# Batched matrix product on one core: load order at the start, stores behind all loads, two outputs in the input's buffers

## The chip, the cores and the metric

The kernel runs on one NeuronCore of a Trainium2 chip. Five engines work side by side: TensorE (PE) multiplies, VectorE (DVE) rounds, transposes and copies, ScalarE (ACT) copies, GpSimd (POOL) does next to nothing here, and SyncE (SP) issues the transfers between the chip's main memory (HBM) and the core's working memory (SBUF). The transfers themselves are carried out by 16 DMA engines. TensorE writes its results into PSUM, a memory of 8 banks[...].

The metric is the device time of one execution in microseconds; lower is better. The profile is of a separate execution, and its span is from the first to the last instruction on the core.

## The reference

```python
def setup_inputs():
    batch, dim_i, dim_j, dim_k = 32, 256, 512, 384
    return {
        "x": np.random.randn(batch, dim_i, dim_j).astype(np.float32),
        "y": np.random.randn(batch, dim_j, dim_k).astype(np.float32),
    }

def reference(x, y):
    return np.einsum('bij,bjk->bik', x, y).astype(np.float32)
```

There are 32 independent products of a 256x512 matrix with a 512x384 matrix. The inputs are 16.8 MB (x) and 25.2 MB (y), the output 12.6 MB.

## The kernel before

Four batch entries form a group, so there are 8 groups, 0 to 7. Each entry of a group takes 32 of the 128 partitions. What is done for a group `n` is split into parts, each with a letter, and a plan lists the parts in program order:

- `x`, `y`: load the group's x (2 MB) or y (3 MB). Both are issued by SP.
- `T`: VectorE rounds x to float16 (one instruction) and transposes it (two instructions, or four for a "wide" group).
- `R`: VectorE rounds y to float16, in four instructions.
- `M`: TensorE multiplies, 128 products in two halves `e` of 64. Half `e` fills four PSUM banks, `(e, 0)` to `(e, 3)`.
- `C`: ScalarE copies banks to the output tile. `D`: VectorE copies the banks that are left to it.
- `S`: SP stores the output tile (1.5 MB).

```python
Q = 4
STEP = 4
O_BUFS = 5
WIDE_GROUPS = 6

PLAN = """
x0 x1 y0
T0 x2 y1
T1 R0 M0 C0 x3 y2
T2 D0 R1 M1 C1 x4 y3
T3 D1 R2 M2 C2 x5 y4
T4 D2 R3 M3 C3 x6 y5
T5 D3 R4 M4 C4 x7 S0 S1 S2 y6
T6 D4 R5 M5 C5 y7
T7 D5 R6 M6 C6 R7 M7 C7 D7 S3 S4 S5 S6 S7
"""
# ... (cut)
    x_pool = ctx.enter_context(tc.tile_pool(name="x_pool", bufs=2))
    y_pool = ctx.enter_context(tc.tile_pool(name="y_pool", bufs=2))
    xr_pool = ctx.enter_context(tc.tile_pool(name="xr_pool", bufs=1))
    xt_pool = ctx.enter_context(tc.tile_pool(name="xt_pool", bufs=3))
    yr_pool = ctx.enter_context(tc.tile_pool(name="yr_pool", bufs=2))
    o_pool = ctx.enter_context(tc.tile_pool(name="o_pool", bufs=O_BUFS))
# ... (cut)
    def width(n):
        return PQ if n < WIDE_GROUPS else 2 * PQ        # PQ = 32

    def on_vector(n, e, g):
        if n < WIDE_GROUPS:
            return (e, g) == (NE - 1, Q - 1)            # NE = 2
        return n == N - 1 and g % 2 == 1                # N = 8

    def load_x(n):
        x_of[n] = x_pool.tile([P, R, J], F32, name="x_sb")
        keep(nc.sync.dma_start(out=x_of[n], in_=x[...]))        # cut

    def transpose_x(n):
        x_r = xr_pool.tile([P, R, J], MM_DT, name="x_r")
        keep(nc.vector.tensor_copy(x_r, x_of.pop(n)))
        # ... transposes of x_r into xt_of[n] (cut)

    def round_y(n):
        y_sb = y_of.pop(n)
        yr_of[n] = yr_pool.tile([P, T, K], MM_DT, name="y_r")
        for a in range(0, T, STEP):                     # T = 16
            keep(nc.vector.tensor_copy(yr_of[n][:, a : a + STEP], y_sb[:, a : a + STEP]))

    def multiply(n):
        # ... (cut)
        o_of[n] = o_pool.tile([P, R, K], F32, name="o_sb")
        for e in range(NE):
            for g in range(Q):
                ps_of[n, e, g] = bank[e, g]
            for t in range(T):
                for g in range(Q):
                    s = slice(g * PQ, (g + 1) * PQ)
                    keep(nc.tensor.matmul(ps_of[n, e, g], xt[s, e, t // 2, :, t % 2], y_r[s, t],
                                          start=(t == 0), stop=(t == T - 1)))
```

A pool with `bufs=2` has two buffers. A new tile gets a buffer whose earlier tile has had its last use in program order, and the first instruction that writes the new tile waits for that use. A load of x is therefore held back by the rounding of an earlier x. Each engine takes its instructions in program order, and SP holds its queue while an issue waits.

A group below `WIDE_GROUPS` has its banks copied in pieces of 32 rows, four a bank; a wide group in pieces of 64 rows, two a bank.

Of the kernel before, what the change touches and what calls it, by code (L numbers as in the profile page):

```python
# [1 line left out]

# [4 lines left out]


MM_DT = mybir.dt.float16
F32 = mybir.dt.float32  # L10
P = 128


Q = 4
STEP = 4
O_BUFS = 5
WIDE_GROUPS = 6

PLAN = """
x0 x1 y0
T0 x2 y1
T1 R0 M0 C0 x3 y2
T2 D0 R1 M1 C1 x4 y3
T3 D1 R2 M2 C2 x5 y4
T4 D2 R3 M3 C3 x6 y5
T5 D3 R4 M4 C4 x7 S0 S1 S2 y6
T6 D4 R5 M5 C5 y7  # L30
T7 D5 R6 M6 C6 R7 M7 C7 D7 S3 S4 S5 S6 S7
"""


@with_exitstack
def kernel(
    ctx: ExitStack,
    tc: tile.TileContext,
    x: bass.AP,
    y: bass.AP,  # L40
    out: bass.AP,
):
    nc = tc.nc

    B, I, J = x.shape
    _, _, K = y.shape

    PQ = P // Q
    R = I // PQ
    T = J // PQ  # L50
    TW = T // 2
    NE = I // P
    N = B // Q
# [7 lines that stand above are left out]
    psum_pool = ctx.enter_context(  # L61
        tc.tile_pool(name="psum", bufs=1, space=bass.MemoryType.PSUM)
    )

    keep = tc.keep_in_program_order

    bank = {
        (e, g): psum_pool.tile([P, K], F32, name=f"o_ps_{e}_{g}") for e in range(NE) for g in range(Q)
    }

    x_of, y_of, xt_of, yr_of, ps_of, o_of = {}, {}, {}, {}, {}, {}

    def width(n):
        return PQ if n < WIDE_GROUPS else 2 * PQ

    def on_vector(n, e, g):
        if n < WIDE_GROUPS:  # L80
            return (e, g) == (NE - 1, Q - 1)
        return n == N - 1 and g % 2 == 1

    def load_x(n):
        x_of[n] = x_pool.tile([P, R, J], F32, name="x_sb")
        keep(
            nc.sync.dma_start(
                out=x_of[n],
                in_=x[n * Q : (n + 1) * Q].rearrange("g (p r) j -> (g p) r j", r=R),
            )  # L90
        )

    def load_y(n):
        y_of[n] = y_pool.tile([P, T, K], F32, name="y_sb")
        keep(
            nc.sync.dma_start(
                out=y_of[n],
                in_=y[n * Q : (n + 1) * Q].rearrange("g (q t) k -> (g q) t k", t=T),
# [8 lines that stand above are left out]
        xt_of[n] = xt_pool.tile([P, NE, TW, P], F32, name="xt_sb")  # L107
        b = width(n) // PQ
        src = x_r.bitcast(F32).rearrange("p (b h e) (q t) -> p b e t h q", b=b, e=NE, t=TW)
        dst = xt_of[n].rearrange("p e t (h s b) -> p b e t h s", s=PQ, b=b)  # L110
        for e in range(NE):
            for c in range(b):
                keep(nc.vector.transpose(dst[:, c, e], src[:, c, e]))  # L113
# [4 lines that stand above are left out]
        for a in range(0, T, STEP):  # L118
            keep(nc.vector.tensor_copy(yr_of[n][:, a : a + STEP], y_sb[:, a : a + STEP]))  # L119

    def multiply(n):
        xt = xt_of.pop(n).bitcast(MM_DT).rearrange("p e t (m c) -> p e t m c", c=2)
        y_r = yr_of.pop(n)
        o_of[n] = o_pool.tile([P, R, K], F32, name="o_sb")
        for e in range(NE):
            for g in range(Q):
                ps_of[n, e, g] = bank[e, g]
# [3 lines that stand above are left out]
                    keep(  # L131
                        nc.tensor.matmul(  # L132
                            ps_of[n, e, g],
                            xt[s, e, t // 2, :, t % 2],
                            y_r[s, t],
                            start=(t == 0),
                            stop=(t == T - 1),
                        )
                    )

    def collect(n, vector):
        w = width(n)
        per = P // w
        copy = nc.vector.tensor_copy if vector else nc.scalar.copy
        o = o_of[n].rearrange("p (u f) k -> p u f k", u=Q // per)
        for e in range(NE):
            for g in range(Q):
                if on_vector(n, e, g) != vector:
                    continue
                ps = ps_of.pop((n, e, g))  # L150
                a = g % per * w
                for h in range(per):
                    keep(copy(o[a : a + w, g // per, h * NE + e], ps[h * w : (h + 1) * w]))  # L153

    def store(n):
        w = width(n)
        per = P // w
        dst = out[n * Q : (n + 1) * Q].rearrange("(u g) (s f) k -> (g s) u f k", g=per, s=w)
        keep(
            nc.sync.dma_start(  # L160
                out=dst, in_=o_of.pop(n).rearrange("p (u f) k -> p u f k", u=Q // per)
            )
        )

    parts = {
        "x": load_x,
        "y": load_y,
        "T": transpose_x,
        "R": round_y,
        "M": multiply,  # L170
        "C": lambda n: collect(n, False),
        "D": lambda n: collect(n, True),
        "S": store,
    }
    for step in PLAN.split():
        parts[step[0]](int(step[1:]))


# [1 line left out]
_INS = ['x', 'y']  # L180
_OUTS = [((32, 256, 384), 'float32')]


# [23 lines left out]
```

## Time and profile before

The device time is 134.45 us (median of 3 runs, 134.24 to 134.48). The span of the profiled execution is 132.9 us.

| Engine | busy us | share of the span | instructions |
|---|---|---|---|
| TensorE, products | 61.5 | 46% | 1024 |
| TensorE, weight loads | 34.9 | 26% | 1024 |
| VectorE | 96.1 | 72% | 92 |
| ScalarE | 91.7 | 69% | 193 |

| Instruction | count | mean ns |
|---|---|---|
| ScalarE copy of a 32x384 piece | 168 | 470 |
| ScalarE copy of a 64x384 piece | 24 | 474 |
| VectorE copy of a piece | 32 | 556 |
| VectorE rounding of a quarter of y | 32 | 953 |
| VectorE rounding of x | 8 | 2292 |
| VectorE transpose of half of x | 12 | 2001 |
| VectorE transpose of a quarter of x | 8 | 1075 |

The DMA engines moved 54.68 MB at a mean of 412 GB/s: 41.94 MB are read from HBM and 12.58 MB written. In the profile's lines L87 is the load of x, L96 the load of y, L106 the rounding of x, L113 its transposition, L119 the rounding of y, L132 the products, L153 the copies out of PSUM and L160 the store. A line of a timeline gives start and duration in us, engine, line, operation, output and input, and in brackets the idle time before it and what ended it. "SPq" is SP issuing a transfer, not the transfer. A row of the slices divides the span into 40 equal parts of 3.3 us; a digit is the busy share in tenths.

### The profile page before, as it was taken

The page shows a single profiled execution, that of the slowest core. Times are in us where ns is not written, and L with a number is a line of the kernel's source. Part 1 is how long each engine was busy: PE and PEld are TensorE (multiplying, and loading weights), DVE is VectorE, ACT ScalarE, POOL GpSimd, SP SyncE. Part 2 cuts the span into 40 slices and gives each one's busy share as a digit, 9 for nine tenths or more (in the row PEclk, how much of TensorE's full clock was granted, in tenths as well). Part 3 has the DMA queues.
Part 4 walks back from the last instruction along what each step waited for, and adds up shares of the span by engine and source line. Part 5 has one row for each costly group of instructions (what it writes and reads, how often), then busy time and mean ns, then how long its engine had stood idle before and what let it go on. Part 6 is the DMA issues. An engine that isn't in the chain of part 4 may idle for free.

```text
span 132.9 us, 2437 instructions
## 1 busy us (share of the span) xinstructions
PE 61.5 (46%) x1024; PEld 34.9 (26%) x1024; DVE 96.1 (72%) x92; ACT 91.7 (69%) x193; POOL 0.2 (0%) x4
## 2 busy tenths in 40 slices
PE   0000004990399129924952395329540079887100
PEld 0000002550147014612541153115320034455000
DVE  0049999699959999999997999699951090735600
ACT  3000000089999999999999999999999961998500
POOL 0000000000000000000000000000000000000000
PEclk9999999999658975797799869985999555999955
DMA  4999999999999999999999999999999999999993
GB/s 109 429 424 441 451 414 429 446 429 412 419 471 407 404 437 441 432 409 446 429 417 414 456 432 402 414 419 429 429 464 429 414 451 400 419 425 412 400 412 141
DMA packets 3723, 54.68 MB, mean 412 GB/s; under 512 B 384, under 2 KB 384, under 8 KB 896
## 3 DMA queue, kind: packets, MB, share of 16 engines
q1 hardware_dynamic: 3712, 54.53, 96.9%
q8 instruction: 8, 0.13, 0.4%
q14 instruction: 3, 0.02, 0.0%
HBM read 41.94 MB, written 12.58 MB: 410 GB/s over the span
## 4 chain that ended last, share of the span: by engine, by line
DMA 45%; DVE 19%; ACT 15%; PE 10%; issue 4%; DVEq 1%
DMA x_sb<-in_x_dram 22%; DMA y_sb<-in_y_dram 22%; ACT o_sb L153 15%; PE o_ps L132 10%; DVE xt_sb L113 6%; DVE x_r L106 5%; DVE o_sb L153 4%; DVE y_r L119 4%; DVEq L202 1%; DVEq L106 0%
## 5 line engine op out<-in xcount | busy, mean ns | idle before, releaser
L153 ACT COPY o_sb<-o_ps 32x384 f32<-32x384 f32 (+1 forms) x192 | 90.4, 471 | 32.7 <-PE o_ps L132 25.8
L132 PE MATMUL o_ps<-y_r,xt_sb 32*128 32x384 f16 x1024 | 61.5, 399 | 61.7 <-DVE y_r L119 52.3
L132 PEld LDWEIGHTS <-xt_sb 32*128 32x128 f16 x1024 | 34.9, 113 | 87.9 <-DVE y_r L119 32.8
L119 DVE CAST y_r<-y_sb 128x1536 f16<-128x1536 f32 x32 | 28.5, 953 | 10.3 <-DMA y_sb<-in_y_dram 10.2
L113 DVE STREAM_TRANSPOSE xt_sb<-x_r 128x1024 f32<-128x1024 f32 (+1 forms) x20 | 31.7, 1631 | 0.3
L106 DVE CAST x_r<-x_sb 128x4096 f16<-128x4096 f32 x8 | 18.3, 2292 | 11.1 <-DMA x_sb<-in_x_dram 11.0
L153 DVE COPY o_sb<-o_ps 32x384 f32<-32x384 f32 (+1 forms) x32 | 17.8, 556 | 7.8 <-PE o_ps L132 3.8
L153 ACT ACT_TABLE_LOAD x1 | 1.3, 1283 | 0.7 <-PEq L191 0.7
L191 POOL MEMSET const-uint8-127<- 128x1 uint8 x1 | 0.1, 103 | 0.0
L191 POOL MEMSET const-bfloat16-1.0<- 128x1 bf16 x1 | 0.1, 102 | 0.0
L191 POOL MEMSET const-float32-0.0<- 128x1 f32 x1 | 0.1, 99 | 0.2 <-issue 0.2
L191 POOL MEMSET const-float32-1.0<- 128x1 f32 x1 | 0.1, 99 | 0.0
## 6 DMA issues: line engine op xcount, KB each, us to landing
y_sb<-in_y_dram SPq DMA_DIRECT2D x8, 3072.0 KB, 21.5
x_sb<-in_x_dram SPq DMA_DIRECT2D x8, 2048.0 KB, 22.0
out_dram<-o_sb SPq DMA_DIRECT2D x8, 1536.0 KB, 25.6
```

Source lines behind the costliest of these rows:

```text
L106: keep(nc.vector.tensor_copy(x_r, x_of.pop(n)))
L113: keep(nc.vector.transpose(dst[:, c, e], src[:, c, e]))
L119: keep(nc.vector.tensor_copy(yr_of[n][:, a : a + STEP], y_sb[:, a : a + STEP]))
L132: nc.tensor.matmul(ps_of[n, e, g], xt[s, e, t // 2, :, t % 2], y_r[s, t], start=(t == 0), stop=(t == T - 1),)
L153: keep(copy(o[a : a + w, g // per, h * NE + e], ps[h * w : (h + 1) * w]))
L191: nc = _bacc.Bacc("TRN2", target_bir_lowering=False, num_devices=1)
L202: with _tile.TileContext(nc) as tc:
```

## The change

The change does four things:

1. **Order at the start.** y and x of groups 0 and 1 are loaded first, each y ahead of its x, and y is rounded before x is transposed.
2. **Stores behind all loads.** Before, the stores of groups 0 to 2 stood between the loads of x7 and y6; now all eight stand behind y7.
3. **Outputs of groups 5 and 6 in x's buffers.** With all stores late, five output buffers no longer suffice. The outputs of groups 5 and 6 are written into buffers of x's pool, which has no more loads to take after x7. Group 7 uses the buffer of group 0's output once that is stored.
4. **Copies of group 6.** Group 6 becomes a narrow group (32-row pieces), and VectorE copies two of its banks, `(1, 2)` and `(1, 3)`; before it copied none of them. In groups 0 to 5 it copies one bank, as before, and in group 7 four.

It aims at an earlier start of the products and at a tail in which the stores run after the loads have ended and the last products overlap with them.

```diff
-WIDE_GROUPS = 6
+WIDE_GROUPS = 7
+
+O_IN_X = (5, 6)
 
 PLAN = """
-x0 x1 y0
-T0 x2 y1
-T1 R0 M0 C0 x3 y2
-T2 D0 R1 M1 C1 x4 y3
-T3 D1 R2 M2 C2 x5 y4
-T4 D2 R3 M3 C3 x6 y5
-T5 D3 R4 M4 C4 x7 S0 S1 S2 y6
-T6 D4 R5 M5 C5 y7
-T7 D5 R6 M6 C6 R7 M7 C7 D7 S3 S4 S5 S6 S7
+y0 x0 y1 x1
+R0 T0 M0 C0 x2 y2
+R1 T1 D0 M1 C1 x3
+T2 D1 R2 M2 C2 x4 y3
+T3 D2 R3 M3 C3 x5 y4
+T4 D3 R4 M4 C4 x6 y5
+T5 D4 R5 M5 C5 x7 y6
+T6 D5 R6 M6 C6 y7 S0 S1 S2 S3 S4
+T7 R7 D6 M7 C7 D7 S5 S6 S7
 """
@@ on_vector
-        if n < WIDE_GROUPS:
-            return (e, g) == (NE - 1, Q - 1)
-        return n == N - 1 and g % 2 == 1
+        if n == N - 1:
+            return g % 2 == 1
+        return e == NE - 1 and g >= (Q - 1 if n < N - 2 else Q - 2)
@@ multiply
-        o_of[n] = o_pool.tile([P, R, K], F32, name="o_sb")
+        if n in O_IN_X:
+            x_sb = x_pool.tile([P, R, J], F32, name="x_sb")
+            o_of[n] = x_sb.rearrange("p r j -> p (r j)")[:, : R * K].rearrange(
+                "p (r k) -> p r k", r=R
+            )
+        else:
+            o_of[n] = o_pool.tile([P, R, K], F32, name="o_sb")
```

## The prediction

> **What bounds the kernel now.** I read the page's 40 slices first (section 2), then the DMA queues (3), the chain (4), and then the timelines of SP, VectorE and ScalarE. The slices show this:
>
> ```profile
> DMA  4999999999999999999999999999999999999993
> GB/s 109 429 424 441 451 414 429 446 429 412 419 471 407 404 437 441 432 409 446 429 417 414 456 432 402 414 419 429 429 464 429 414 451 400 419 425 412 400 412 141
> ...
> q1 hardware_dynamic: 3712, 54.53, 96.9%
> ...
> DMA 45%; DVE 19%; ACT 15%; PE 10%; issue 4%; DVEq 1%
> ```
>
> Every slice but the first and last has the DMA engines 90% busy or more, at 400 to 471 GB/s; the one queue that moves the tensors fills 96.9% of 16 engines' span. The chain names DMA for only 45%, because it walks through whichever wait ended last, but the queue behind it never runs dry. So **the kernel is bound by its DMA stream**: a new order of the same bytes can gain almost nothing, and any hole in the stream is paid in full.
>
> Issue times plus times to landing (DMA view, asked around each issue) give the stream: x0 issued 0.73, landed 8.4; x1 at 13.3; y0 at 20.6; later x6 at 53.83 + 22.0 = 75.8, y5 at 63.71 + 19.4 = 83.1, x7 at 66.03 + 21.9 = 88.0, and the last store at 125.58 + 6.5 = 132.1. From neighbours, one x load takes 4.9 us (13.3 - 8.4; 88.0 - 83.1), one y load 7.3 us (20.6 - 13.3; 83.1 - 75.8). x0, on an empty queue, took 7.65 us: **2.75 us more than its data**.
>
> The second view is how far ahead the loads are issued, on SP's queue:
>
> ```profile
> 63.72 0.33 SPq L96 DMA_DIRECT2D y_sb<-in_y_dram  x1
> 66.03 0.33 SPq L87 DMA_DIRECT2D x_sb<-in_x_dram  x1
> 66.41 1.80 SPq L160 DMA_DIRECT2D out_dram<-o_sb  x3
> 76.62 13.93 SPq L96 DMA_DIRECT2D y_sb<-in_y_dram  x2
> 90.64 35.31 SPq L160 DMA_DIRECT2D out_dram<-o_sb  x5
> ```
>
> y5 and x7 are issued at 63.7 and 66.0, when the engines still have y4 (lands at 70.9) and x6 to move. y6 can only go at 76.6 and y7 at 90.2, when their buffers come free; the three stores at 66.4 put 10.9 us of work into the queue (the third lands at 67.88 + 31.0 = 98.9, x7 had at 88.0; 3.65 us each) and bridge that.
>
> The third view is the pace of the computing engines:
>
> ```profile
> 27.09 81.51 ACT L153 COPY o_sb<-o_ps 32x384 f32<-32x384 f32 x168 [25.08 <-PE o_ps L132]
> ...
> 84.32 2.26 DVE L153 COPY o_sb<-o_ps 32x384 f32<-32x384 f32 x4 [1.42 <-PE o_ps L132]
> 86.61 3.57 DVE L119 CAST y_r<-y_sb 128x1536 f16<-128x1536 f32 x4
> 90.10 2.29 DVE L106 CAST x_r<-x_sb 128x4096 f16<-128x4096 f32 x1
> ```
>
> ScalarE, once started at 27.09, copies for 81.5 us without a break: 168 copies, 0.485 us each, 28 a group, so **13.6 us a group**. VectorE follows it: its own copies of group 4 start at 84.32, when the matmuls, which wait for ScalarE to empty PSUM banks, are done; then 2.3 us of copies, 3.6 us of y5's rounding and 2.3 us of x7's rounding, to 92.4: 8.1 us in a row.
>
> **What the Trainium skill says.** "DMA: Bandwidth & Descriptors", section "Anatomy of one DMA": a semaphore wait happens on the issuing sequencer before dispatch; the DMA engines only consume their queues. So a load that waits holds back all that SP has behind it; the trace agrees (stores L160 at 90.64 come straight after y7's load, which waited until 90.2). The same section gives about 2.0 us of fixed cost a DMA, for another path; x0 shows 2.75 here, and I use that. "Perfetto Trace Analysis", section "Identifying the Most-Contended Engine", says occupancy of DMA misleads and to use bandwidth: here both say the same, 96.9% and 412 GB/s. Its section "Optimization Strategy" says gaps can mean too few buffers; before has none in the DMA row, so no run here shows it yet.
>
> **The change part by part.**
>
> 1. Start. y0 (7.3 us) now lands before x0: y0 at 8.4 - 4.9 + 7.3 = 10.8, x0 at 15.7. y0 is rounded under x0's transfer. Then x0's rounding (2.3) and first transpose (1.95): TensorE starts at 20.0, not 21.78. Its first half group took 27.09 - 21.78 = 5.3 us; I keep that. ScalarE starts at about 25.3 instead of 27.1: **1.8 us earlier**. y1 and x1 land by 27.9; x1's rounding and first transpose end at 32.2, group 1's first half is multiplied by about 38.4, before ScalarE ends group 0 at 25.3 + 13.6 = 38.9, so ScalarE stays unbroken.
>
> 2. Stores behind all loads. The three stores that stood between x7 and y6 move behind y7. No bytes are saved.
>
> 3. Outputs in x's buffers. There are two x buffers. In the changed program the output of group 5 is taken ahead of x7, and gets the buffer of x5; x7 is left with that of **x6**, and its load waits for x6's rounding, where before it waited for x5's. In VectorE's order that rounding stands behind the copies of group 4 and the rounding of y5. y6, y7 and all eight stores stand behind x7 on SP.
>
> 4. When is x7 issued? VectorE's copies of group 4 move with ScalarE: 84.3 - 1.8 = 82.5. Then the 8.1 us above (2.3 copies, 3.6 y5, 2.3 now of x6): **x7 at about 90.6**. y5 itself does not move: the same 13 loads lie up to its end, so it lands at 83.1 in any order, and its rounding at 84.8 need not wait. Loads before it stay ahead: x6 and y5 go out at about 65, with y4 in flight until 71. So the engines have nothing from 83 on.
>
> 5. The sum. x7 lands at 90.6 + 7.65 = 98.25, against 88.0 before: **10.3 us later**. Behind it is the same work as before, 2 y loads and 8 stores, which took 132.1 - 88.0 = 44.1 us without a hole. The end is at 98.25 + 44.1 = 142.3 if none opens there. Adding the difference to the measured time: 134.45 + 10.3 = **144.7 us**.
>
> 6. The tail. From 98.25, y6 lands at 105.6, y7 at 112.9; five stores then carry the stream to 131.2, the sixth to 134.9, the seventh to 138.6. VectorE: y6 to 109.2, x7's rounding and four transposes (2.3 + 4.1) to 115.6, y7 to 119.2, eight copies of 0.57 to 123.7. ScalarE: 24 narrow copies of group 6 take 11.6 us where 16 wide ones took 7.8, from 112 to 123.6. So store 6 is ready at 123.7 and is only needed at 134.9. Group 7: first half multiplied from 119.7 (banks empty) to 125.0, second to 127.9, copies to 130.2; needed at 138.6. Both have over 8 us to spare: the narrow copies of group 6 and the two banks given to VectorE cost and gain nothing.
>
> **The rivals.**
>
> - **The stream stays full.** Then the time is that of before, about 134.4, since the bytes are the same; even the last store's wait of a tail transfer is no gain, as the DMA rows are full up to it. For it speaks only that all loads before x7 do stay ahead. Against it: x7's load would have to be issued by about 81, and VectorE's row puts x6's rounding 10 us later.
> - **A shorter tail wins.** The chain before ends with y7 landing at 113.7, multiplication, copies and one store. With stores last, this lies under 29 us of stores. It would show if the DMA row had a hole between 114 and 126; slices there read 9 and 400 to 425 GB/s. At most 1 us: 133.5.
> - **ScalarE or VectorE becomes the bound in the tail**, with group 6 in 32-row pieces. ScalarE has 200 copies, 97 us, from 25.3; idle waits included it ends near 130 in step 6. It would need 8 us more than I count to be seen.
> - **The hole is smaller.** With y5's landing at 83.1 as the only limit, x7 could go at 83.1 + 3.6 + 2.3 = 89.0, if TensorE's first half were quicker and ScalarE ran further ahead: -1.6 us. If a restarted queue needs 0.7 us less than x0 did at launch, -0.7 us. Together 142.4. Upward: one of the engines can fall behind the others after the restart, or ScalarE breaks off once or twice; I allow 2 us.
>
> **Range and chances.** Centre 144.7; 142.4 to 147.0 holds both directions. Slower than 137.1 (2%) fails only if the buffers don't bind as in step 3, and that follows from the program's order, not from a duration: 0.96 slower, 0.03 within 2%, 0.01 faster.
>
> **What would show it.** After: the DMA row falls to near nothing for three slices around 83 to 92; SP's longest wait is that of an x load (about 25 us, from 65) for VectorE's rounding of x6; the issue there at 90 to 91; its landing near 98; ScalarE's first copy at 25.3; DMA full from 93 to the end; ScalarE idle about 5 us ahead of group 6. Wrong would be: x7 issued before 83 (step 3 falls), ScalarE's start not near 25.3 (step 1), or a second hole behind 98 (step 6).

## The result and the profile after

The changed kernel takes **146.88 us** (median of 6 runs, 146.5 to 147.9) against 134.43 us before. The ratio is 1.0946, with a 95% interval of 1.0903 to 1.0988: 12.5 us slower, where 10.3 were predicted. The span of the profiled execution grows from 132.9 to 144.8 us, by 11.9.

The page of the changed kernel: DMA row, rate, queue and chain.

```profile
DMA  5999999999999999999999300899999999999992
GB/s 170 428 416 441 441 423 419 426 441 439 405 426 426 453 428 407 441 421 421 437 428 435 127 0 0 254 432 428 435 435 350 419 420 431 424 429 424 428 413 90
...
q1 hardware_dynamic: 3584, 54.53, 89.9%
...
ACT 42%; DMA 21%; PE 14%; DVE 10%; issue 2%; SPq 0%; DVEq 0%
```

A slice is now 3.62 us. Slices 22 to 25 (counted from 0), 80 to 94 us, hold the hole; two of them move nothing at all. The same 54.53 MB fill 89.9% of the span instead of 96.9%. The chain names ScalarE first although it lost nothing of its own: its copies set the time at which VectorE reached x6's rounding, and that released x7.

SP's queue in the timeline of the changed kernel (start, duration, line, operation, output and input, count):

```profile
64.04 0.33 SPq L89 DMA_DIRECT2D x_sb<-in_x_dram  x1
64.42 0.42 SPq L98 DMA_DIRECT2D y_sb<-in_y_dram  x1
90.17 0.33 SPq L89 DMA_DIRECT2D x_sb<-in_x_dram  x1
90.55 0.90 SPq L98 DMA_DIRECT2D y_sb<-in_y_dram  x2
91.49 2.81 SPq L168 DMA_DIRECT2D out_dram<-o_sb  x5
```

x6 and y5 go out at 64; then SP issues nothing for 26 us. At 90.17 x7 goes, and y6, y7 and five stores, which by then have next to nothing to wait for, follow within some 4 us. They had all stood behind x7. The trace agrees here with what the Trainium skill says of waits on the issuing sequencer ("DMA: Bandwidth & Descriptors", "Anatomy of one DMA").

What x7 waited for is in VectorE's timeline of the changed kernel:

```profile
82.08 2.27 DVE L161 COPY o_sb<-o_ps 32x384 f32<-32x384 f32 x4 [1.53 <-PE o_ps L140]
84.37 3.57 DVE L121 CAST y_r<-y_sb 128x1536 f16<-128x1536 f32 x4
87.86 2.28 DVE L108 CAST x_r<-x_sb 128x4096 f16<-128x4096 f32 x1
```

Copies of group 4, y5's rounding, x6's rounding: 82.08 to 90.14, and x7 is issued at 90.17. The first line's bracket says that the copies waited 1.53 us for products, so VectorE was not behind; it kept ScalarE's pace.

### The profile page after: what moved, and what is told of

It reads as the page before. It is cut to its first block, busy times and chain, and to the rows that moved or that the text cites. A ratio compares the mean times of both kernels' runs of the same rounds, so it can differ in the third digit from the quotient of the medians.

```text
span 144.8 us, 2445 instructions
## 1 busy us (share of the span) xinstructions
PE 65.1 (45%) x1024; PEld 36.4 (25%) x1024; DVE 100.2 (69%) x98; ACT 95.2 (66%) x201; POOL 0.2 (0%) x4
## 3 DMA queue, kind: packets, MB, share of 16 engines
q1 hardware_dynamic: 3584, 54.53, 89.9%
## 4 chain that ended last, share of the span: by engine, by line
ACT 42%; DMA 21%; PE 14%; DVE 10%; issue 2%; SPq 0%; DVEq 0%
ACT o_sb L161 36%; PE o_ps L140 14%; DMA y_sb<-in_y_dram 11%; DMA x_sb<-in_x_dram 10%; ACT x_sb L161 5%; DVE y_r L121 3%; DVE x_r L108 3%; DVE o_sb L161 2%; DVE xt_sb L115 1%; DVEq L210 0%; SPq L98 0%; SPq L89 0%; DVEq L161 0%
## 5 line engine op out<-in xcount | busy, mean ns | idle before, releaser
L140 PE MATMUL o_ps<-y_r,xt_sb 32*128 32x384 f16 x1024 | 65.1, 415 | 61.9 <-DVE y_r L121 29.0
L161 ACT COPY o_sb<-o_ps 32x384 f32<-32x384 f32 (+1 forms) x148 | 69.5, 470 | 26.1 <-PE o_ps L140 23.6
L140 PEld LDWEIGHTS <-xt_sb 32*128 32x128 f16 x1024 | 36.4, 116 | 90.2 <-DVE y_r L121 31.3
L161 ACT COPY x_sb<-o_ps 32x384 f32<-32x384 f32 x52 | 24.4, 470 | 6.7 <-PE o_ps L140 6.0
L161 DVE COPY o_sb<-o_ps 32x384 f32<-32x384 f32 (+1 forms) x28 | 15.6, 556 | 3.2 <-PE o_ps L140 2.4
L161 DVE COPY x_sb<-o_ps 32x384 f32<-32x384 f32 x12 | 6.7, 555 | 1.7 <-PE o_ps L140 1.5
```

## The experiments

Each kernel is one edit of the changed kernel ("after") or of the one before. The first four vary the time at which x7 is issued. e2 and e3 also put off group 5's products, and e4 VectorE's later work; by the prediction's step 6 there is slack for that.

**e1: x7 taken ahead of the output of group 5.** Two buffers swap owners, nothing else.

```diff
-T5 D4 R5 M5 C5 x7 y6
+T5 D4 R5 x7 M5 C5 y6
```

> The changed kernel with one thing moved in the plan: x7 is taken ahead of the output of group 5, so x7 gets the buffer of x5 and the output that of x6. Everything else of the change stays (stores last, outputs in x's buffers, narrow group 6). My theory (the whole loss is the hole ahead of x7): x7 is issued at about 76.6, when x5 is rounded, the stream has no hole, and the time is that of before, 134.4 us within 1. Rival (stores last, or outputs in x's buffers, cost by themselves): it stays above 140 us.

Measured: 134.34 us, ratio to before 0.9993 (0.9985 to 1.0000). From the page of e1:

```profile
DMA  4999999999999999999999999999999999999993
```

And from SP's timeline of e1:

```profile
77.34 0.33 SPq L89 DMA_DIRECT2D x_sb<-in_x_dram  x1
77.72 11.31 SPq L98 DMA_DIRECT2D y_sb<-in_y_dram  x2
89.08 4.78 SPq L168 DMA_DIRECT2D out_dram<-o_sb  x5
```

x7 goes 12.8 us earlier, the row is full, and all of the loss is gone. So neither stores behind all loads nor outputs in x's buffers cost anything by themselves. The last load of y lands at 102.5 instead of 113.7 in the kernel before, and that brings nothing either.

**e2: x6 rounded ahead of VectorE's copies of group 4.**

```diff
-T5 D4 R5 M5 C5 x7 y6
-T6 D5 R6 M6 C6 y7 S0 S1 S2 S3 S4
+T5 T6 D4 R5 M5 C5 x7 y6
+D5 R6 M6 C6 y7 S0 S1 S2 S3 S4
```

> The changed kernel with x6's rounding and transposes moved ahead of VectorE's copies of group 4, so that x7, still bound to x6's buffer, is issued at about 82.9 instead of 90.2. If each us of x7's issue is paid in full, counted from the first of the 16 DMA engines that runs dry (about 80): 146.9 - 7.3 = 139.6 us. If only the slowest engine counts, which runs dry about 2 us later, as in my prediction's step 5: x7 lands at 82.9 + 7.65 = 90.5, 2.5 later than in the kernel before, so 136.9 us. Rival of a hole that is hidden while it is short: 134.4.

Measured: 140.07 us, ratio 1.0435 (1.0401 to 1.0468).

**e3: x6 rounded ahead of y5.**

```diff
-T5 D4 R5 M5 C5 x7 y6
-T6 D5 R6 M6 C6 y7 S0 S1 S2 S3 S4
+T5 D4 T6 R5 M5 C5 x7 y6
+D5 R6 M6 C6 y7 S0 S1 S2 S3 S4
```

> The changed kernel with x6's rounding and transposes between VectorE's copies of group 4 and y5's rounding: x7 is issued at 84.4 + 2.3 = 86.7, 3.5 us earlier. Paid in full: 146.9 - 3.5 = 143.4 us. Group 5's products start some 6 us later, which uses up the idle time of ScalarE ahead of group 6, and costs nothing if the tail has the slack that I counted; a rival with a tight tail expects less gain, 145 to 147.

Measured: 143.47 us, ratio 1.0667 (1.0638 to 1.0696).

**e4: y5 rounded twice, into the same tile.**

```diff
-        for a in range(0, T, STEP):
+        for a in [*range(0, T, STEP)] * (2 if n == 5 else 1):
```

> The changed kernel with y5 rounded twice into the same tile (four instructions more, the same result), so that x6's rounding and x7's issue come 3.6 us later, at 93.7. Paid in full: 146.9 + 3.6 = 150.5 us. Rival (the loss is not the hole but a fixed cost of the restart or of the tail): 147.

Measured: 148.99 us, ratio 1.1093 (1.1053 to 1.1133). This is the median of three runs, 148.57 to 150.02; a fourth, 152.23, fell in a slower state of the chip and is not counted. The rival's 147 is too low.

The four kernels with a hole, with the issue of x7 read from SP's timelines. The lines of e2, e3 and e4, in this order:

```profile
83.37 0.33 SPq L89 DMA_DIRECT2D x_sb<-in_x_dram  x1
86.83 0.33 SPq L89 DMA_DIRECT2D x_sb<-in_x_dram  x1
93.15 0.33 SPq L89 DMA_DIRECT2D x_sb<-in_x_dram  x1
```


| Kernel | x7 issued | time, us | time minus issue |
|---|---|---|---|
| e2 | 83.37 | 140.07 | 56.70 |
| e3 | 86.83 | 143.47 | 56.64 |
| after | 90.17 | 146.88 | 56.71 |
| e4 | 93.15 | 148.99 | 55.84 |

**Each microsecond by which x7 is issued later costs about a microsecond:** from e2 to e4 the issue moves by 9.8 us and the time by 8.9. No part of the hole is hidden, even when it is short: e2 issues x7 2.6 us after the first DMA engine ran dry (80.8) and 0.3 after the last (83.1), and loses 5.7 us. My sum has 54.1 in the last column (134.45 + 7.65 - 88.0): it is short by 2.5 to 2.6 us in the first three and by 1.7 in e4. Taken from the slowest engine as the prediction did, e2 should have been at 136.9; 139.6, from the engine that runs dry first, was close.

**e5: the first three stores back ahead of x7.** x7 still waits for x6's buffer.

```diff
-T5 D4 R5 M5 C5 x7 y6
-T6 D5 R6 M6 C6 y7 S0 S1 S2 S3 S4
+T5 D4 R5 M5 C5 S0 S1 S2 x7 y6
+T6 D5 R6 M6 C6 y7 S3 S4
```

> The changed kernel with the stores of groups 0, 1 and 2 put back ahead of x7, as the kernel before has them; x7 still waits for x6's buffer. They put 10.9 us of work into the queue behind y5, up to about 93.9, and x7 is issued at 90.2: no hole there. Only five stores are left for the end: the store of group 6 is ready at 123.9 and wanted at 124.4, too late to be ahead of the queue, that of group 7 at 129.3, so it lands at about 129.3 + 6.5 = 135.8 against 132.1 before. My theory: 138 us, of which all above 134.4 is this tail. Rival (the late x7 itself, or the buffers, cost): above 143.

Measured: 138.59 us, ratio 1.0301 (1.0284 to 1.0319). From the page of e5, and x7 in its SP timeline:

```profile
DMA  5999999999999999999999999999999999995756
...
89.70 0.34 SPq L89 DMA_DIRECT2D x_sb<-in_x_dram  x1
```

With x7 still issued at 89.7 the middle of the row is full: a late load costs only if nothing lies in the queue ahead of it. The last four slices show the other end of the trade. Five stores are not enough to cover the last products, and the stores of groups 6 and 7 go out at 124.25 and 130.43 into a queue that has run dry.

**e6: the new start order alone, in the kernel before.** Stores 0 to 2 stay ahead of y6, outputs have their own five buffers.

```diff
-x0 x1 y0
-T0 x2 y1
-T1 R0 M0 C0 x3 y2
... (cut)
+y0 x0 y1 x1
+R0 T0 M0 C0 x2 y2
+R1 T1 D0 M1 C1 x3
... (cut; then as in the change, but:)
+T5 x7 S0 S1 S2 D4 R5 M5 C5 y6
+T6 y7 T7 D5 R6 M6 C6 R7 M7 C7 D7 S3 S4 S5 S6 S7
```

> The kernel before with the first part of the change alone: y and x of groups 0 and 1 first, y rounded ahead of x, and the plan drawn up from there; stores 0 to 2 still ahead of y6, outputs in their own five buffers, group 6 wide. ScalarE starts 2 us earlier, but the bytes and a full queue decide: 134.4 us within 0.7. Rival (an earlier start shortens the whole): 132.5.

Measured: 134.38 us, ratio 1.0001 (0.9988 to 1.0015). ScalarE's first copy comes at 24.34 instead of 27.09, and the time stays: an earlier start of computing is worth nothing beside a full stream.

**e7: group 6 narrow, in the kernel before**, with two of its banks on VectorE (`WIDE_GROUPS = 7`, the new `on_vector`, and `R7 D6 M7` in the plan).

> The kernel before with the fourth part of the change alone: group 6 narrow, two of its banks copied by VectorE. In the kernel before, the tail behind y7 is followed at once by the last store. Group 7's first half waits until the first four banks of group 6 are empty: 16 copies of 0.485 instead of 8, 3.9 us later; the last store is issued at 129.5 instead of 125.6 and lands at about 136: 138.3 us. Rival (the last store has slack, or the two banks on VectorE make up for it): 134.4.

Measured: 137.36 us, ratio 1.0221 (1.0193 to 1.0249): slower by 3.0 us, 3.9 expected. Stretches of 2 us at the end of e7 (stretch, length, busy time and count of PE, PEld, DVE, ACT and POOL, then clock, DMA share and GB/s):

```profile
122.00:124.00 2.00, 2.00 (x35) 1.13 (x28) 0.00 (x0) 1.08 (x3) 0.00 (x0) 0.53 0.54 227
...
128.00:130.00 2.00, 0.00 (x0) 0.00 (x0) 1.11 (x2) 0.68 (x2) 0.00 (x0) 1.00 0.03 8
```

The last two stores come too late, and the DMA engines wait for them.

**e8: group 6 wide again, in the changed kernel** (the old `on_vector`, `WIDE_GROUPS = 6`).

> The changed kernel with the fourth part undone: group 6 wide again and all its banks on ScalarE. By step 6 of my prediction the stores of groups 6 and 7 are ready some 8 us before the queue comes to them, so the time stays at 146.9 us within 0.7. Rival (the narrow copies are part of the 12 us lost): 143 to 145.

Measured: 147.3 us, ratio 1.0959 (1.0922 to 1.0997), no different from after. The copies of group 6 that cost 3 us in e7 cost nothing here, since five stores lie in the queue ahead. This is step 6 of the prediction.

**e9 and e10: what a part of the 2.5 us is.** The trace has 16 completion events for each transfer, one for each DMA engine; "first", "mean" and "last" are of these 16, and a load's time is counted from the completion of the transfer ahead of it. In after, e2, e3, e4 and e8, which have a hole, y7, the last load ahead of the stores, took 7.9 to 8.1 us in the mean, against 7.3 and 7.4 in before and e1. e9 puts a store between y6 and y7, e10 takes x7's rounding away from beside y7's transfer.

```diff
 e9:
-T6 D5 R6 M6 C6 y7 S0 S1 S2 S3 S4
+T6 D5 R6 M6 C6 S0 y7 S1 S2 S3 S4
 e10:
-T7 R7 D6 M7 C7 D7 S5 S6 S7
+R7 T7 D6 M7 C7 D7 S5 S6 S7
```

> The changed kernel with the store of group 0 between the loads of y6 and y7. In every kernel with a hole so far, y7, the last load ahead of the stores, took about 8.0 us (mean over the 16 engines) instead of 7.3, with slow packets on nearly all engines in its last 2 us; in the kernels without a hole it took 7.3. Theory A: after the hole all 16 engines are in step and pass from reading to writing HBM at once, which costs about 0.7 us: then y6 takes 8.0 here, and its slow packets come near 104. Theory B: x7's rounding on VectorE, which runs from 109.4 to 111.7, slows the transfers beside it: then y6 takes 7.3 and the slow packets stay near 110. Time in both: 147 us, A up to 0.7 more for a second passage.

> The changed kernel with x7's rounding and transposes behind y7's rounding on VectorE, so that no rounding of x runs beside y7's load: it moves from 109.4 to about 118. Theory A (all engines pass from loads to stores in step): y7 still takes about 8.0 us. Theory B (x7's rounding slows y7's transfer): y7 takes 7.3 us. Group 7 gets ready some 6 us later; the last store is then issued at about 135.5, against 137.5 at the latest by my count, so the time stays near 146.9 us; if the tail has less slack than I counted, it rises above 148.

Measured: e9 147.35 us, ratio 1.0941 (1.0896 to 1.0986); e10 147.08 us, ratio 1.0942 (1.0926 to 1.0958). In e9 the slow load is now y6, 7.9 us, and y7 takes 7.0; in e10 y7 still takes 7.9. Stretches of e9, columns as above:

```profile
102.00:104.00 2.00, 0.00 (x0) 0.00 (x0) 0.00 (x0) 1.94 (x5) 0.00 (x0) 0.50 0.94 369
104.00:106.00 2.00, 0.00 (x0) 0.00 (x0) 0.00 (x0) 1.93 (x5) 0.00 (x0) 0.50 0.99 320
106.00:108.00 2.00, 0.00 (x0) 0.00 (x0) 0.00 (x0) 0.89 (x2) 0.00 (x0) 0.50 0.98 418
114.00:116.00 2.00, 2.00 (x48) 1.06 (x44) 1.97 (x3) 0.94 (x3) 0.00 (x0) 0.79 0.91 393
116.00:118.00 2.00, 1.60 (x40) 0.76 (x32) 2.00 (x3) 1.94 (x5) 0.00 (x0) 1.00 0.90 381
```

And of e10:

```profile
108.00:110.00 2.00, 2.00 (x32) 0.99 (x28) 1.87 (x3) 0.00 (x0) 0.00 (x0) 0.50 1.05 418
110.00:112.00 2.00, 2.00 (x32) 0.92 (x28) 0.00 (x0) 0.00 (x0) 0.00 (x0) 0.50 0.79 240
```

In e9 the dip lies at 102 to 106, where VectorE does nothing, and goes with the passage from loads to stores. In e10 it lies at 110 to 112 with VectorE idle as well. So x7's rounding (theory B) is out, and the dip goes with the passage.

That the passage costs something because the engines are in step is **not shown, and two measurements speak against it**. For it: one load ahead of the passage the mean engine is 0.35 to 0.5 us behind the first in the kernels with a hole, and 0.75 or more in those without. Against it: e9 passes from loads to stores a second time, at 116, with the mean engine still 0.4 behind, and pays nothing. The store of group 0 and y7 together take 10.9 us in the mean there, as much as a store and a load elsewhere (3.65 and 7.3), and the stretches from 114 to 118 show no such dip. And e5, with no hole ahead of x7 and the mean engine 1.1 us behind, has y7 at 7.5 us, with slow packets at 110 to 112. What the runs show is a loss of 0.6 to 0.8 us, once, in the last load ahead of the first stores behind a hole; its cause stays open.

## Why the prediction was right or wrong

**Direction and cause: right.** Step 3 named the buffer and the instruction that holds x7. e1 takes that one binding away and the whole loss goes.

**Step 1, the start: right.** First copy of ScalarE at 24.96 (25.3 predicted), and unbroken through group 5:

```profile
24.96 67.80 ACT L161 COPY o_sb<-o_ps 32x384 f32<-32x384 f32 x140 [22.96 <-PE o_ps L140]
92.78 13.53 ACT L161 COPY x_sb<-o_ps 32x384 f32<-32x384 f32 x28
112.31 11.61 ACT L161 COPY x_sb<-o_ps 32x384 f32<-32x384 f32 x24 [5.99 <-PE o_ps L140]
```

The third line of this ScalarE timeline of after has the 6 us of idle time ahead of group 6 that were foreseen as 5.

**Step 4, the issue: right.** y5 landed at 83.0 (83.1), x7 was issued at 90.17 (90.6). Where I foresaw one wait of SP of about 25 us, its waits show two: 10.9 us for x6 to land, at 75.7, and this line for its rounding (total, times, longest):

```profile
SPq L89 <- DVE x_r L108: 41.5, 6, 14.4
```

**Step 5, the sum: the step that failed, mis-sized by 1.6 us in the profiled run.** Issue 0.4 earlier; landing 8.6 after issue instead of 7.65 (0.9 more); and 45.2 us from x7's landing to the last store's instead of 44.1 (1.1 more). The times to landing of x7 and of the last store (issued at 129.26) in after:

```profile
x_sb<-in_x_dram SPq DMA_DIRECT2D x1, 2048.0 KB, 8.6
out_dram<-o_sb SPq DMA_DIRECT2D x1, 1536.0 KB, 14.7
```

The term that is too small in every kernel with a hole is the 44.1, "the same work as before". In the two kernels with a full stream and the four with a hole it measures:

| Kernel | x7 landed after issue | x7's landing to the last store's | of the first engine alone | spread of the engines, at x7 and at the end |
|---|---|---|---|---|
| before | queued | 44.1 | 44.7 | 2.1, 1.5 |
| e1 | queued | 43.8 | 43.7 | 2.1, 2.2 |
| e2 | 7.7 | 46.3 | 44.6 | 0.9, 2.6 |
| e3 | 7.6 | 47.0 | 44.5 | 0.7, 3.1 |
| after | 8.6 | 45.2 | 44.5 | 1.5, 2.2 |
| e4 | 7.7 | 45.4 | 44.8 | 0.8, 1.5 |

I had treated the stream as one server, timed at the last of its 16 engines. In the kernel before, that engine came into the stretch 2.1 us behind the first, and the 44.1 us hold no more falling behind. A hole lets the late ones catch up, so it is longer for the first engine (dry from about 80, not 83), and they fall apart once more behind it: 0.6 to 2.4 us. On the first engine alone the stretch is 0.8 to 1.1 us longer behind a hole (44.5 to 44.8 against 43.7 in e1; in before, the first engine's 44.7 has a wait for the last store's issue in it), of which y7 ahead of the stores is 0.6 to 0.8. The 7.65 for a restart was right in e2 to e4; in after one engine lands late. A 16 KB packet of the queue of instructions starts at 96.7 there, while x7 is under way. e8, e9 and e10 have such a packet at 96.4 to 97.3 and land x7 8.9 to 9.1 us after issue; e2, e3 and e4 have none while x7's data move. The link holds in all seven, but no run varied the packets. The remaining 0.6 us is between the medians (12.5) and the spans (11.9). I had allowed 2 us upward for engines that fall behind, as a chance; engines fell behind in every kernel with a hole. That put the median, 146.88, at the very top of the range (147.0), and the ratio of 1.0946 times the time before, 147.1, just above it.

**Step 6, the tail: right.** Store of group 6 issued at 123.9 (123.7), that of group 7 at 129.3 (130.2), both far ahead of the queue. e8 confirms the slack. e10 uses it up: it issues the last store 9 us later, at 138.5, about a microsecond past the latest time of my count, and its time rises by only 0.2. Most engines do wait for that store, which takes 5.2 us in the mean instead of 3.7, but the last engine, 3.1 us behind the first, has work up to 140.8 and sets the end.

**The rivals.** "The stream stays full" is e1. "A shorter tail wins" failed: e1 and e6 have an earlier start, e1 also an early last load, and both give the time of before. A tail bound by the last copies was seen only in e5 and e7, where five stores are left behind the loads. "The hole is smaller" failed: x7 was issued at 90.17 and not at 89.0, and no restart took less than 7.6 us.

## What to carry to other kernels

In a kernel whose DMA row is full, look for the one load whose buffer is freed latest, and at all that stands behind it on its queue. A tile borrowed from a load's pool took the buffer that came free next, and the order in which two tiles were taken was worth 9% here (146.88 against 134.34 us). A late issue is harmless while earlier work lies in the queue (e5). In the four kernels of the table it costs the time from when the first DMA engine runs dry, at 80.6 to 80.8, to the issue, plus 2.2 to 3.1 us for the restart and what follows it. Here, moving stores to the end bought slack for the tail and took away the filler in the middle; check both ends.

## What was not expected

- The 16 DMA engines drift apart by about 2 us from first to last and stay so. The drift's steps fall together with fetches of instructions, 16 KB packets on a queue of their own. In before, of the loads up to x7, just y1, x4, x5, x6 and x7 take 0.09 us or more (up to 0.12, in the mean of the engines) longer than their like; if one engine of 16 bears it, that is 1.4 to 1.9 us for it. One such packet starts during each of the five (30.5, 45.5, 58.2, 71.6, 85.4). No run varied the fetches. A hole brings most of them back together: in after, the mean engine is 0.96 us behind the first at y5 and 0.35 at x7; by the end it is 0.66.
- Behind a hole, the first passing from loads to stores costs about 0.7 us over all engines (7.9 to 8.1 us for the last load instead of 7.3). Without a hole it costs at most 0.2 (e5), and a second passage in e9 costs nothing that can be seen.
- No order tried beat the kernel before: 134.34 (e1) and 134.38 us (e6). With 54.53 MB at some 425 GB/s in the full slices, fewer bytes or a shorter ramp at the ends are what is left, unless that rate can be raised, which no run here tried.
